# A hybrid HGRN2 and stick-breaking block: FFN and embedding stores issued on ScalarE's DMA queue

## The chip, the cores and the metric

The kernel runs on one core of a Trainium2 chip. The core has TensorE (PE in the profile, with PEld for its weight loads), VectorE (DVE), ScalarE (ACT), GpSimd (POOL) and SyncE (SP), and 16 DMA engines that serve all of its queues. The metric is the device time of one execution in microseconds; the time before is the median of three runs.

## The reference

One layer of a decoder trunk on 2048 tokens of width 1024. What is computed, cut to its core:

```python
u = rmsnorm(h, attn_pre_norm)
hq, hf, hi, hg, sq, sk, sv = split(u @ w_in)
o_hg = rmsnorm(hgrn2_mix(hq, hf, hi, lb), hg_out_norm) * silu(hg)    # 4 heads, recurrent
o_sb = rmsnorm(stick_breaking_mix(sq, sk, sv), sb_out_norm)          # 8 heads, causal
h = h + rmsnorm(concat([o_hg, o_sb]) @ w_out, attn_post_norm)
u = rmsnorm(h, ffn_pre_norm)
gate, up = split(u @ w_gate_up)                                      # 1024 -> 2 x 2816
y = (silu(gate) * up) @ w_down                                       # 2816 -> 1024
h = h + rmsnorm(y, ffn_post_norm)
h = h + (p @ ple_proj) * sigmoid(h @ ple_gate)                       # p: 2048 x 256
```

All of it is in float32. The change touches what comes behind the attention heads: part of the residual before the feed-forward network (FFN), the FFN, and the gated per-layer embedding.

## The kernel before

**Stages.** The first 1500 us hold the input projection, the two kinds of heads and most of the output projection. Behind them a `Drive` runs six lists of steps in order: `gate_up(0)`, `down(0)`, `gate_up(1)`, `down(1)`, `ple(0)`, `ple(1)`. The number is a pair of token groups (1024 tokens, in two groups of 512). Each step has a `prepare` (loads and splits of weights) and a `run` (matmuls); `Drive` prepares three to five steps ahead. Side work hangs on the steps as hooks: `post_late` (residual of the last group, L717), `turner` (transposes of normalised rows, L752), `down_combos` and `ple_combos` (combinations of weight blocks, L834), `make_pt` (transposes of `p`, L775), `post_y` and `turn_y` (residual of the FFN and its transposes, L1079 and L1089).

**Arithmetic.** A float32 matrix product is done with three matmuls of rounded operands: `pair_of` has ScalarE round a tile (`wh` or `uh`, L811), and VectorE or GpSimd takes the remainder (`wl` or `ul`, L812); `mm3` issues the three matmuls (L223 to L225). Each large product goes block by block with the seven products of a Strassen-like scheme, in the order 1, 2, 6, 3, 7, 5, 4 (`CHAIN`); `chain` adds them up from PSUM. The blocks' sums and differences go through the helpers `sub` and `add`, so they appear as L816 and L819.

**What passes through DRAM.** `gate_up` works in 11 column blocks for each pair; at the end of each block it forms the seven operands of the hidden layer that `down` needs and stores them in `hid_s` (five at L1016, two at L1021). `down_combos` and `ple_combos` store the combinations of `w_down` and `ple_gate`. `post_y` stores the residual stream in `h2_s`, `turn_y` its transposes in `h2t_s`, and `ple` the result.

**Queues and order.** Every DMA, load or store, is issued by SyncE in one order. Weights and reloaded tiles come through `load` (L796) into 12 slots `wr`; a load waits until its slot is free, which is when the last operation on the tile before is done, mostly the subtraction of L812. TensorE's order is that of the program. The order of the other engines, and each DMA's completion semaphore out of eight, is set by the framework's scheduler as it builds the program. A DMA waits for what it reads or overwrites, and for the landing of the DMA that used its semaphore before.

**PSUM.** TensorE's transposes in `turner`, `make_pt` and in `turn_y` for one group of each pair share one bank, `hg`. ScalarE takes their result out (L751 for `turner`, L1088 for `turn_y`), and the next transposes wait for that.

Of the kernel before, what the change touches and what calls it, by code (L numbers as in the profile page):

```python
# [15 lines left out]
P = 128  # L16
# [72 lines left out]
def hybrid_block(  # L89
# [6 lines left out]
    nc = tc.nc  # L96
    ctx.enter_context(tc.manual_schedule(engines={mybir.EngineType.PE}))
    x, p, out = x[0], p[0, 0], out[0]
# [16 lines left out]
    h_s = scratch("h_s", (GT, D))  # L115
    h2_s = scratch("h2_s", (GT, D))
# [3 lines left out]
    pt_s = scratch("pt_s", (PLE // P, P, GT))  # L120
# [8 lines left out]
    def ctile(name, shape, dt=F32, pool=const):  # L129
# [9 lines left out]
        out=maskneg, in_=maskneg, compare_op=ALU.is_gt, fill=-1e30, base=0,  # L139
# [566 lines left out]
    def post_late(g):  # L706

        for t in range(TT):
            rows = slice(t * P, (t + 1) * P)
            ss = const.tile([P, 2], F32, tag="ss", name="ss", bufs=8)  # L710
            for j in range(2):
                cs = slice(j * GT, (j + 1) * GT)
                m, h = load(h2_s[g][rows, cs]), load(x[g * GT + t * P:g * GT + (t + 1) * P, cs])
                gb = load(attn_post_norm[0:1][:, cs].to_broadcast((P, GT)))
                nc.vector.scalar_tensor_tensor(m, m, rows_m[t], gb, op0=ALU.mult, op1=ALU.mult)
                nc.gpsimd.tensor_tensor(h, h, m, op=ALU.add)
                nc.sync.dma_start(h_s[g][rows, cs], h)  # L717
                nc.scalar.activation(junk, h, AF.Square, accum_out=ss[:, j:j + 1])
                if j == 1:
                    row_rstd(None, rows_h[t], ss)  # L720
                yield

    def turn(src, dst, gain, tag, new_in, new_out, scales=None):

        def get(q):
            ts = []
            for i in range(2):
                r = new_in().rearrange("p (t d) -> p t d", t=2)
                rows = src[2 * i * P:2 * (i + 1) * P, q * 256:(q + 1) * 256]
                nc.sync.dma_start(r, rows.rearrange("(t p) d -> p t d", p=P))  # L730
                for n in range(2):
                    if scales:
                        nc.scalar.activation(r[:, n, :], r[:, n, :], AF.Copy, scale=scales[2 * i + n])
                    ts.append(r[:, n, :])
            return ts

        nxt = get(0)
        yield
        for q in range(4):
            ts = nxt  # L740
            nxt = get(q + 1) if q < 3 else None
            for c in range(2):
                b = bank(tag)
                for t in range(TT):
                    nc.tensor.transpose(b[:, t * P:(t + 1) * P], ts[t][:, c * P:(c + 1) * P], ident)
                e = new_out()
                k = 2 * q + c
                if gain is None:
                    nc.scalar.copy(e, b)
                else:  # L750
                    nc.scalar.activation(e, b, AF.Copy, scale=gain[:, k:k + 1])  # L751
                nc.sync.dma_start(dst[k], e)  # L752
                yield

    def make_pt():
        def get(n):
            raw = load(p[2 * n * P:2 * (n + 1) * P, :].rearrange("(t p) d -> p t d", p=P),
                       lambda r: r.rearrange("p (t d) -> p t d", t=2))
            return raw.rearrange("p (t d) -> p t d", t=2)

        nxt = get(0)
        yield
        for n in range(NG * TT // 2):
            raw = nxt
            nxt = get(n + 1) if n + 1 < NG * TT // 2 else None
            b = bank("hg")
            for t in range(2):
                for c in range(PLE // P):
                    nc.tensor.transpose(
                        b[:, (c * 2 + t) * P:(c * 2 + t + 1) * P], raw[:, t, c * P:(c + 1) * P], ident)  # L770
            e = acc("pt")
            nc.scalar.copy(e, b)
            g, i = divmod(n, TT // 2)
            for c in range(PLE // P):
                nc.sync.dma_start(pt_s[g][c][:, 2 * i * P:2 * (i + 1) * P], e[:, c * 2 * P:(c + 1) * 2 * P])  # L775
            yield


# [51 lines left out]
    def combos(blk, dst, e):  # L830
        t = [load(blk(i, j)) for i, j in ((0, 0), (0, 1), (1, 0), (1, 1))]
        b_combos(*t, e)
        for i, r in zip((1, 3, 4, 2), t):
            nc.sync.dma_start(dst[i - 1], r)  # L834

    wd_s = [dram.tile([4, P, GT], F32, tag=f"wd_s{k}", name=f"wd_s{k}") for k in range(DFF // 256)]
    wp_s = [dram.tile([4, P, GT], F32, tag=f"wp_s{k}", name=f"wp_s{k}") for k in range(ND // 2)]
# [115 lines left out]
    def gate_up(grp, tt):  # L953
        def block(fb):
            s = {}
            cs = [{}, {}]

            def wload(i, j):
                out = []
                for n in range(2):  # L960
                    r = slice((4 * j + 2 * n) * P, (4 * j + 2 * n + 2) * P)
                    c0 = i * DFF + fb * 256
                    out.append(load(w_gate_up[r, c0:c0 + 256].rearrange("(k p) n -> p k n", p=P),
                                    lambda r: r.rearrange("p (k n) -> p k n", k=2)))
                return out

            def prepare(prod):
                if prod == 1:
                    w = wload(0, 0)
                elif prod == 2:  # L970
                    w = wload(0, 1)
                elif prod == 6:
                    w, a21, a22 = wload(0, 0), wload(1, 0), wload(1, 1)
                    s["s1"] = [xt("s1") for _ in range(2)]
                    s["s3"] = [xt("s3") for _ in range(2)]
                    for n in range(2):
                        add(V, s["s1"][n], a21[n], a22[n])
                        sub(V, s["s3"][n], w[n], a21[n])
                        sub(V, w[n], s["s1"][n], w[n])
                    s["s2"] = w  # L980
                elif prod == 3:
                    w = wload(0, 1)
                    for n in range(2):
                        sub(V, w[n], w[n], s["s2"][n])
                elif prod == 7:
                    w = s["s3"]
                elif prod == 5:
                    w = s["s1"]
                else:
                    w = wload(1, 1)  # L990
                s[prod] = [pair_of(t, "w", prod, V if n or prod in (6, 3) else G) for n, t in enumerate(w)]

            def gated(j):
                for q in range(2):
                    sg = acc("sg")
                    nc.scalar.activation(sg, cs[q][1, j], AF.Sigmoid)
                    nc.vector.tensor_tensor(sg, cs[q][1, j], sg, op=ALU.mult)
                    nc.vector.tensor_tensor(cs[q][2, j], cs[q][2, j], sg, op=ALU.mult)

            def run(prod):  # L1000
                for q in range(2):
                    b = mm_bank()
                    for k in range(ND // 2):
                        o = (k % 2) * 256 + q * P
                        mm3(b, [t[:, o:o + P] for t in s[prod][k // 2]], tt[prod, k], k == 0, k == ND // 2 - 1)
                    chain(prod, cs[q], b, new_gu)
                if prod == 5:
                    gated(2)
                if prod == 4:
                    gated(1)  # L1010
                    h11, h12, h21, h22 = cs[0][2, 1], cs[1][2, 1], cs[0][2, 2], cs[1][2, 2]
                    s1, s3 = acc("hs"), acc("hs")
                    add(V, s1, h21, h22)
                    sub(V, s3, h11, h21)
                    for i, t in ((1, h11), (2, h12), (4, h22), (5, s1), (7, s3)):
                        nc.sync.dma_start(hid_s[grp][fb, i - 1], t)  # L1016
                    s2, s4 = acc("hs"), acc("hs")
                    sub(V, s2, s1, h11)
                    sub(V, s4, h12, s2)
                    for i, t in ((6, s2), (3, s4)):  # L1020
                        nc.sync.dma_start(hid_s[grp][fb, i - 1], t)  # L1021

            return {prod: (lambda p=prod: prepare(p), lambda p=prod: run(p)) for prod in CHAIN}

# [45 lines left out]
    def post_y(g, i):  # L1070
        halves = ready[g][i]
        r = row_rstd(halves)
        for j, t in enumerate(halves):
# [2 lines left out]
            nc.vector.scalar_tensor_tensor(t, t, r, gy, op0=ALU.mult, op1=ALU.mult)  # L1076
            hr = load(h_s[g][i * P:(i + 1) * P, cs])
            add(G, t, t, hr)
            nc.sync.dma_start(h2_s[g][i * P:(i + 1) * P, cs], t)  # L1079

    def turn_y(g, i, tag):

        for j, t in enumerate(ready[g][i]):
            b = bank(tag)
            for c in range(TT):
                nc.tensor.transpose(b[:, c * P:(c + 1) * P], t[:, c * P:(c + 1) * P], ident)
            e = acc("ht")
            nc.scalar.copy(e, b)  # L1088
            nc.sync.dma_start(  # L1089
                h2t_s[g][TT * j:TT * (j + 1), :, i * P:(i + 1) * P].rearrange("k p t -> p k t"),  # L1090
                e.rearrange("p (k t) -> p k t", k=TT))

# [1 line left out]
    def ple(grp, ss):  # L1094
# [29 lines left out]
        def run_p(half, i):  # L1124
            for j in range(2):
# [7 lines left out]
                hr = load(h2_s[g0 + half][i * P:(i + 1) * P, c])  # L1133
                add(G, y, y, hr)
                r0 = (g0 + half) * GT + i * P
                nc.sync.dma_start(out[r0:r0 + P, c], y)

        def none():
            pass
# [154 lines left out]
        return slot("wr", 0, "wr")  # L1294

    def turner(src, dst, gain, scales=None):
        return turn(src, dst, gain, "hg", wr, acc, scales)

    for k in range(ND // 2):
        at(0, k, lambda k=k: t_second(0, tt0, k))  # L1300
# [48 lines left out]
```

## Time and profile before

| what | value |
|---|---|
| median of three runs | 3060.1 us (3058.16 to 3062.44) |
| the profiled execution's own time | 3057.24 us |
| its span | 3055.5 us |
| granted TensorE clock | 0.99 |
| DMA, mean over the span | 197 GB/s |
| chain that ended last | PE 41%, DMA 6%, DVE 5%, POOL 3%, issue 3%, ACT 1% |

The page is read from the busy shares of the engines to the stretches of time in which they stand idle. `L834 <- DVE wr L816: 34.9, 28, 3.9` in a list of waits means: ahead of line 834 the engine named first was idle for 34.9 us in all, 28 times, 3.9 us at the longest, and what ended it was VectorE's operation of line 816 on tile `wr`. In a timeline a row gives start, duration, engine, line, operation, output and inputs, and in brackets the idle time before it with its releaser. In a table by windows, the busy time of PE, PEld, DVE, ACT and POOL is followed by the granted clock (1.00 is full speed), the busy share of the 16 DMA engines and what they moved. The costliest groups of the page, to show the form (busy time, mean ns of one, idle time before and its main releaser):

```profile
L811 ACT CAST wh<-wr 128x512 fp32r<-128x512 f32 x600 | 352.8, 618 | 473.4 <-PE mm L224 192.5
L812 POOL TENSOR_TENSOR wl<-wr,wh 128x512 fp32r<-128x512 f32 x256 | 370.6, 1453 | 460.8 <-ACT wh L811 427.1
L223 PE MATMUL mm<-uh,wh 128*128 128x512 f32 x1168 | 482.4, 413 | 1.9 <-DVE eb L336 1.6
```

### The profile page before, as it was taken

The numbers are of one execution on the slowest core, as the hardware profiler recorded it, in microseconds if no ns is written. First come the engines' busy times: TensorE is split into PE (matmuls) and PEld (weight loads), VectorE is DVE, ScalarE is ACT, GpSimd is POOL, SyncE is SP. The second block draws the span as 40 slices with busy tenths as digits, with TensorE's granted clock in tenths as the row PEclk, the third lists the DMA queues.
The fourth block names the chain that finished last, engine by engine and source line by source line (L and its number), as shares of the span: only waits on it lengthen the run. The fifth ranks groups of instructions, "written<-read, shape, count | busy, mean of one in ns | idle before, by whom it ended". The sixth has DMA issues, their size and how long they took to land.

```text
span 3055.5 us, 52953 instructions
## 1 busy us (share of the span) xinstructions
PE 2920.4 (96%) x18280; PEld 2425.4 (79%) x18280; DVE 2065.6 (68%) x2917; ACT 1583.7 (52%) x3188; POOL 1463.9 (48%) x1490
## 2 busy tenths in 40 slices
PE   8999999999999998888998999999999999999989
PEld 6888787878787787778886878888788888878767
DVE  3556666677677776745787787655877776656674
ACT  5666656666666666757633233455433333545442
POOL 3344455545556665857522223455732221456564
PEclk9999999999999999999999999999999999999999
DMA  7765565455445444447867767667955555677974
GB/s 216 219 213 164 160 183 164 145 158 164 142 139 155 143 136 135 158 154 253 302 213 236 263 211 248 215 196 220 340 188 169 173 172 175 209 217 244 309 248 138
DMA packets 469420, 602.28 MB, mean 197 GB/s; under 512 B 43168, under 2 KB 277664, under 8 KB 469152
## 3 DMA queue, kind: packets, MB, share of 16 engines
q1 hardware_dynamic: 469152, 598.91, 61.9%
q8 instruction: 144, 2.36, 0.3%
q14 instruction: 124, 1.02, 0.1%
HBM read 439.89 MB, written 158.86 MB: 196 GB/s over the span
## 4 chain that ended last, share of the span: by engine, by line
PE 41%; DMA 6%; DVE 5%; POOL 3%; issue 3%; ACT 1%; SPq 0%; POOLq 0%; ACTq 0%; DVEq 0%
PE mm L223 6%; PE mm L224 6%; PE mm L225 6%; PE z L225 4%; PE z L223 4%; PE z L224 4%; PE tr L223 2%; PE tr L224 2%; PE tr L225 2%; PE av L225 2%; PE av L224 2%; PE av L223 2%; DMA wr<-in_w_gate_up_dram 1%; DVE wr L816 1%; DMA wr<-in_ffn_post_norm_dram 1%
## 5 line engine op out<-in xcount | busy, mean ns | idle before, releaser
L811 ACT CAST wh<-wr 128x512 fp32r<-128x512 f32 x600 | 352.8, 618 | 473.4 <-PE mm L224 192.5
L812 POOL TENSOR_TENSOR wl<-wr,wh 128x512 fp32r<-128x512 f32 x256 | 370.6, 1453 | 460.8 <-ACT wh L811 427.1
L435 POOL TENSOR_TENSOR a<-be,ring 128x512 f32<-128x512 f32 (+2 forms) x320 | 318.4, 995 | 431.0 <-DVE ring L431 410.5
L223 PE MATMUL mm<-uh,wh 128*128 128x512 f32 x1168 | 482.4, 413 | 1.9 <-DVE eb L336 1.6
L225 PE MATMUL mm<-uh,wl 128*128 128x512 f32 x1168 | 458.9, 393 | 0.0
L224 PE MATMUL mm<-ul,wh 128*128 128x512 f32 x1168 | 457.1, 391 | 0.0
L812 DVE TENSOR_TENSOR wl<-wr,wh 128x512 fp32r<-128x512 f32 x344 | 299.2, 877 | 181.8 <-ACT wh L811 166.1
L431 DVE TENSOR_TENSOR_SCAN ring<-z,ring,be 128x512 f32<-128x512 f32 x192 | 245.6, 1279 | 114.6 <-ACT z L417 111.6
L223 PE MATMUL mm<-wh,uh 128*128 128x256 f32 (+1 forms) x992 | 308.6, 311 | 1.0 <-DVE vv L350 1.0
L224 PE MATMUL mm<-wl,uh 128*128 128x256 f32 (+1 forms) x992 | 293.7, 296 | 6.7 <-POOL wl L812 6.7
L225 PE MATMUL mm<-wh,ul 128*128 128x256 f32 (+1 forms) x992 | 293.6, 296 | 0.0
L225 PEld LDWEIGHTS mm<-uh,wl 128*128 128x128 f32 x1168 | 219.4, 188 | 50.6
L223 PEld LDWEIGHTS mm<-uh,wh 128*128 128x128 f32 x1168 | 220.5, 189 | 43.7 <-DVE eb L336 2.1
L448 DVE TENSOR_TENSOR al<-tr,ah 128x512 fp32r<-128x512 f32 (+1 forms) x320 | 192.1, 600 | 91.4 <-ACT ah L446 90.8
L224 PEld LDWEIGHTS mm<-ul,wh 128*128 128x128 f32 x1168 | 220.8, 189 | 39.4
L209 ACT CAST wh<-wr 128x512 fp32r<-128x512 f32 x288 | 178.2, 619 | 133.9 <-PE mm L224 80.2
L210 POOL TENSOR_TENSOR wl<-wr,wh 128x512 fp32r<-128x512 f32 x144 | 188.9, 1311 | 100.2 <-ACT wh L209 97.0
L812 POOL TENSOR_TENSOR wl<-s,wh 128x512 fp32r<-128x512 f32 x44 | 97.0, 2211 | 270.8 <-ACT wh L811 242.0
L446 ACT CAST ah<-tr 128x512 fp32r<-128x512 f32 (+1 forms) x320 | 167.6, 524 | 110.6 <-PE tr L443 107.9
L416 ACT ACTIVATE be<-z 128x512 f32<-128x512 f32 (+2 forms) x320 | 171.0, 535 | 90.4 <-PE z L410 40.6
L224 PEld LDWEIGHTS mm<-wl,uh 128*128 128x128 f32 x992 | 191.9, 193 | 12.2 <-POOL wl L812 7.1
L223 PEld LDWEIGHTS mm<-wh,uh 128*128 128x128 f32 x992 | 191.5, 193 | 9.1 <-issue 1.2
(305 smaller groups left out, 7270.0 us busy)
## 6 DMA issues: line engine op xcount, KB each, us to landing
wr<-in_w_gate_up_dram SPq DMA_DIRECT2D x308, 256.0 KB, 3.7
wr<-in_w_in_dram SPq DMA_DIRECT2D x224, 256.0 KB, 3.1
wr<-hid_s SPq DMA_DIRECT2D x154, 256.0 KB, 2.9
wr<-in_w_down_dram SPq DMA_DIRECT2D x110, 256.0 KB, 3.4
hid_s<-hs SPq DMA_DIRECT2D x88, 256.0 KB, 3.5
wr<-wd_s SPq DMA_DIRECT2D x88, 256.0 KB, 3.1
kt<-k_s SPq DMA_DIRECT2D x80, 256.0 KB, 3.0
vt<-v_s SPq DMA_DIRECT2D x80, 256.0 KB, 3.2
```

What stands on the lines that cost most here:

```text
L209: nc.scalar.copy(hi, src)
L210: (lo_engine or nc.gpsimd).tensor_tensor(lo, src, hi.bitcast(F32), op=ALU.subtract)
L223: nc.tensor.matmul(o, l[0], r[0], start=start, stop=False)
L224: nc.tensor.matmul(o, l[0], r[1], start=False, stop=False)
L225: nc.tensor.matmul(o, l[1], r[0], start=False, stop=stop)
L416: nc.scalar.activation(be[:, :n], z[:, :n], AF.Sigmoid, scale=0.125)
L431: nc.vector.tensor_tensor_scan(r[:, o:o + n][:, ::-1], z[:, :n][:, ::-1], be[:, :n][:, ::-1], init, op0=ALU.mult, op1=ALU.bypass)
L435: nc.gpsimd.tensor_tensor(a[:, :n], be[:, :n], r[:, o + 1:o + n + 1], op=ALU.mult)
L446: nc.scalar.copy(hi[:, lo_c:], tr[:, lo_c:])
L448: nc.vector.tensor_tensor(lo[:, lo_c:], tr[:, lo_c:], hi[:, lo_c:].bitcast(F32), op=ALU.subtract)
L811: nc.scalar.copy(hi, src)
L812: lo_engine.tensor_tensor(lo, src, hi.bitcast(F32), op=ALU.subtract)
```

## The change

Ten edits replace SyncE as the issuer of stores by ScalarE. `turn` gets a parameter for it, which `turner` sets; the calls of `turn` in the output projection keep SyncE.

```diff
@@ post_late @@
-                nc.sync.dma_start(h_s[g][rows, cs], h)
+                nc.scalar.dma_start(h_s[g][rows, cs], h)
@@ turn @@
-    def turn(src, dst, gain, tag, new_in, new_out, scales=None):
+    def turn(src, dst, gain, tag, new_in, new_out, scales=None, store=nc.sync):
...
-                nc.sync.dma_start(dst[k], e)
+                store.dma_start(dst[k], e)
@@ make_pt @@
-                nc.sync.dma_start(pt_s[g][c][:, 2 * i * P:2 * (i + 1) * P], e[:, c * 2 * P:(c + 1) * 2 * P])
+                nc.scalar.dma_start(pt_s[g][c][:, 2 * i * P:2 * (i + 1) * P], e[:, c * 2 * P:(c + 1) * 2 * P])
@@ combos @@
-            nc.sync.dma_start(dst[i - 1], r)
+            nc.scalar.dma_start(dst[i - 1], r)
@@ gate_up, run @@
                     for i, t in ((1, h11), (2, h12), (4, h22), (5, s1), (7, s3)):
-                        nc.sync.dma_start(hid_s[grp][fb, i - 1], t)
+                        nc.scalar.dma_start(hid_s[grp][fb, i - 1], t)
...
                     for i, t in ((6, s2), (3, s4)):
-                        nc.sync.dma_start(hid_s[grp][fb, i - 1], t)
+                        nc.scalar.dma_start(hid_s[grp][fb, i - 1], t)
@@ post_y @@
-            nc.sync.dma_start(h2_s[g][i * P:(i + 1) * P, cs], t)
+            nc.scalar.dma_start(h2_s[g][i * P:(i + 1) * P, cs], t)
@@ turn_y @@
-            nc.sync.dma_start(
+            nc.scalar.dma_start(
@@ ple, run_p @@
-                nc.sync.dma_start(out[r0:r0 + P, c], y)
+                nc.scalar.dma_start(out[r0:r0 + P, c], y)
@@ turner @@
-        return turn(src, dst, gain, "hg", wr, acc, scales)
+        return turn(src, dst, gain, "hg", wr, acc, scales, nc.scalar)
```

SyncE issues 2442 DMAs before and 2092 now; 350 go to ScalarE. TensorE's order is the same. Three places of ScalarE's order follow, as pieces of the difference (+ is new; the numbers in names tell tiles apart).

First, ScalarE in `gate_up(0)`, near 1670 us of the profile, where a block of the hidden layer ends; `hs` are its sums, `acc` a transposed tile of `turner`, `s1` and `s3` sums of weights:

```order
 L811 CAST wh_21422<-s3_21300 128x512
+L1016 DMA hid_s0_111<-cu_20987 128x512
 L926 COPY cu_21416<-z_21403 128x512
+L1016 DMA hid_s0_111<-cu_21002 128x512
+L834 DMA wd_s3_239<-wr_21520 128x512
+L1016 DMA hid_s0_111<-hs_21351 128x512
+L1016 DMA hid_s0_111<-hs_21352 128x512
+L834 DMA wd_s3_239<-wr_21518 128x512
 L811 CAST wh_21478<-s1_21297 128x512
+L1021 DMA hid_s0_111<-hs_21360 128x512
 L751 ACTIVATE acc_21371<-hg_21366,g_ffn_172 128x512
```

Five stores of the hidden layer and two of `wd_s` now stand between the cast `wh_21422` and the eviction of the bank `hg` at L751.

Second, ScalarE at the end of `down(0)`, near 2185 us; `c22` and `cu` are the residual tiles that GpSimd's addition completes, `ht` their transposes:

```order
 L811 CAST wh_26371<-s1_26195 128x512
+L1079 DMA h2_s1_92<-cu_24282 128x512
 L811 CAST wh_26375<-s1_26196 128x512
+L1079 DMA h2_s1_92<-c22_25775 128x512
+L1079 DMA h2_s1_92<-cu_24287 128x512
+L1079 DMA h2_s1_92<-c22_25781 128x512
 L1088 COPY ht_26434<-hg_26429 128x512
+L1079 DMA h2_s1_92<-cu_24292 128x512
+L1089 DMA h2t_s1_104<-ht_26434 128x4x128
 L1088 COPY ht_26442<-hg_26437 128x512
```

Four stores of residual tiles, of later rows than those being transposed, now come ahead of the first eviction `ht_26434`.

Third, ScalarE at the end of `down(1)`, near 2843 us, with the same names for the other pair; the activation of L1130 is a sigmoid of `ple`:

```order
 L926 COPY cu_32529<-mm_32516 128x512
+L1079 DMA h2_s3_94<-cu_30490 128x512
 L926 COPY cu_32590<-av_32577 128x512
+L1079 DMA h2_s3_94<-c22_31984 128x512
+L1079 DMA h2_s3_94<-cu_30495 128x512
 L1088 COPY ht_32634<-hg_32629 128x512
 L1130 ACTIVATE c11_32627<-c11_32627 128x512
 L811 CAST wh_32555<-wr_32553 128x512
```

Here three stores come ahead of the first eviction `ht_32634`.

## The prediction

> **What bounds the kernel now.** I read the page's first part, then the windows by stage, then the waits of SyncE's queue and of TensorE, then the timeline where TensorE stands still.
>
> ```profile
> span 3055.5 us, 52953 instructions
> PE 2920.4 (96%) x18280; PEld 2425.4 (79%) x18280; DVE 2065.6 (68%) x2917; ACT 1583.7 (52%) x3188; POOL 1463.9 (48%) x1490
> ```
>
> TensorE is busy for 96% of the span. The first store that changes queue is issued at about 1540 us, so what counts is the time behind 1497 us.
>
> ```profile
> 1497.00:1800.00 303.00, 282.08 (x1208) 227.91 (x1207) 251.78 (x356) 95.97 (x179) 84.10 (x65) 0.96 0.71 229
> 1800.00:2212.00 412.00, 408.13 (x1810) 331.93 (x1809) 285.09 (x385) 190.29 (x352) 201.90 (x142) 1.00 0.74 240
> 2212.00:2620.00 408.00, 408.00 (x1788) 333.17 (x1787) 306.18 (x456) 132.16 (x223) 105.75 (x63) 1.00 0.55 179
> 2620.00:2870.00 250.00, 243.89 (x1077) 196.56 (x1077) 146.92 (x171) 130.46 (x246) 148.41 (x120) 1.00 0.77 247
> 2870.00:3056.00 186.00, 171.39 (x722) 136.85 (x720) 116.00 (x148) 63.19 (x112) 100.36 (x71) 0.97 0.61 204
> ```
>
> The columns are window, length, busy time of PE, PEld, DVE, ACT and POOL, granted clock, DMA share, GB/s. TensorE's idle time here is 20.9 + 3.9 + 0 + 6.1 + 14.6 = 45.5 us. The clock costs 303×0.04 + 186×0.03 = 17.7 us more (an estimate). So at most some 63 us can be won; nothing of the kind limits what can be lost. ScalarE is busy for 612 of these 1559 us.
>
> Does SyncE's order of stores hold its loads back? Its waits, from 1497 us on (total, times, longest):
>
> ```profile
> SPq L796 <- DVE wl L812: 305.0, 249, 6.8
> SPq L796 <- POOL wl L812: 245.3, 159, 10.2
> SPq L834 <- DVE wr L816: 34.9, 28, 3.9
> SPq L1016 <- DVE c L998: 17.1, 17, 3.1
> SPq L1021 <- DVE hs L816: 15.9, 19, 2.5
> ```
>
> Loads (L796) wait 550 us for a free `wr` slot, which the subtraction at L812 gives back. The largest rows of stores sum to 68 us; a load behind such a store would often have met a slot wait next. So the queue is mostly held by slots, not by stores.
>
> **The change, part by part.** 350 stores leave SyncE for ScalarE: 60 of L834, 154 of the hidden products (110 L1016, 44 L1021), 32 each of L1079, L1089 and L1136, 16 each of L752 and L775, 8 of L717. Each carries its wait with it. On SyncE a store that waits for VectorE or GpSimd holds only loads; on ScalarE, which takes its instructions in order, it holds the casts (L811) and the evictions of PSUM behind it. In the built program each DMA also waits for the landing of the previous one on its completion semaphore, and eight of these serve both queues.
>
> *Issuing itself.*
>
> ```profile
> 1682.51 0.43 SPq L1021 DMA_DIRECT2D hid_s<-hs  x1
> 2188.20 0.38 SPq L1079 DMA_DIRECT2D h_s<-c  x1
> 1776.84 2.85 SPq L834 DMA_DIRECT2D wd_s<-wr  x3
> ```
>
> One costs SyncE 0.38 to 0.95 us; ScalarE's price is not in this trace. I take 0.4, so 350 × 0.4 = 140 us beside ScalarE's 947 idle us: nothing by itself. At 0.95 it would be 330 us, still inside, but each burst of four then holds an eviction by 2 us more; that end goes into the upper bounds below.
>
> *Casts held in gate_up.* In the blocks the order puts stores that wait for VectorE ahead of casts. The worst one:
>
> ```profile
> 1762.98 0.62 ACT L811 CAST wh<-wr 128x512 fp32r<-128x512 f32 x1
> 1779.86 0.68 DVE L816 TENSOR_TENSOR wr<-wr 128x512 f32<-128x512 f32 x1
> 1786.78 0.39 PE L223 MATMUL mm<-uh,wh 128*128 128x512 f32 x1
> ```
>
> This cast comes behind three stores of L834, which need the combinations that end near 1779.3, and so falls some 16.7 us later; GpSimd's L812 then ends near 1782. Matched in program order, the first matmul that uses it starts at 1786.78. Covered, with about 4 us left. Other casts slip by 5 us or so against leads of 13 to 20. I charge +2 for the stretch (0 to +8).
>
> *Place A, the one long gap.* L1016 and L1021 stand ahead of the L751 eviction.
>
> ```profile
> 1677.43 0.69 ACT L751 ACTIVATE acc<-hg,g_ffn 128x512 f32<-128x512 f32 x1 [5.68 <-DVE cu L998]
> 1678.17 1.11 PE L745 MATMUL hg<-ident,wr 128*128 128x128 f32 x4 [10.31 <-ACT acc L751]
> 1680.93 0.68 DVE L816 TENSOR_TENSOR hs<-hs,cu 128x512 f32<-128x512 f32 x1
> 1650.00:1700.00 50.00, 39.69 (x173) 32.22 (x172) 34.73 (x51) 14.83 (x28) 10.78 (x10) 0.90 0.72 236
> ```
>
> TensorE waits 10.31 us for the single `hg` bank. The store ahead of that eviction needs the `hs` that ends at 1681.61, so the eviction starts at about 1681.95 in place of 1677.43: +4.5. Earlier loads take back up to 2.8. I take **+3** (0 to +5).
>
> *Place B, the transition from down(0) to gate_up(1).* Ahead of `ht_26434` now stand L1079 stores, which need GpSimd's adds.
>
> ```profile
> 2186.64 0.59 ACT L1088 COPY ht<-hg 128x512 f32<-128x512 f32 x1 [4.29 <-PE hg L1086]
> 2187.37 0.63 PE L1086 MATMUL hg<-ident,c 128*128 128x128 f32 x4 [0.77 <-ACT ht L1088]
> 2187.82 1.30 POOL L819 TENSOR_TENSOR cu<-cu,wr 128x512 f32<-128x512 f32 x1 [0.63 <-DVE cu L1076]
> 2190.41 1.29 POOL L819 TENSOR_TENSOR c<-c,wr 128x512 f32<-128x512 f32 x1 [1.29 <-DVE c L1076]
> 2180.00:2190.00 10.00, 9.23 (x45) 7.48 (x44) 10.00 (x10) 3.52 (x7) 7.86 (x6) 1.00 1.02 335
> ```
>
> The second of these adds ends at 2191.70, its store is issued by 2192.05, and the eviction follows: 5.4 us behind 2186.64. TensorE's next step is four transposes into the bank that it frees, so the 5.4 show in full. The later pairs share this lag rather than add to it. But VectorE is busy for all of the 10 us, and what slips on ScalarE (casts, whose results VectorE and GpSimd take) can slip a second time: 10.8. I take **+9** (+3 to +11), nearer to the upper end because no engine here has slack to catch up with.
>
> *Place C, down(1) to ple(0)*, is built in the same way, with less before it.
>
> ```profile
> 2843.72 0.59 ACT L1088 COPY ht<-hg 128x512 f32<-128x512 f32 x1 [2.64 <-PE hg L1086]
> 2843.48 1.72 POOL L819 TENSOR_TENSOR cu<-cu,wr 128x512 f32<-128x512 f32 x1
> 2840.00:2850.00 10.00, 8.29 (x44) 6.57 (x44) 6.20 (x8) 5.59 (x11) 9.38 (x7) 1.00 1.05 383
> hid_s<-hs SPq DMA_DIRECT2D x88, 256.0 KB, 3.5
> h2t_s<-ht SPq DMA_DIRECT2D x32, 256.0 KB, 5.5
> ```
>
> The add ends at 2845.20, so the first eviction moves by at least 1.8 us. If its store must also await a landing of its semaphore's previous DMA, issued near 2844 and 3.5 to 5.5 us under way, by about 4 or more. GpSimd is at 94%, so a second slip is likely here too: **+6** (+2 to +12).
>
> *The clock.* Place A's gap goes with a granted clock of 0.90 over 50 us, so 5 us lost. New gaps of about half that length at B and C may drop it once, or in several places: **+5** (0 to +15). The Trainium skill, "TensorE: Matmul & The Clock Gate", "Part 1: The HAM clock gate", says that an idle window of about 3.4 us halves the clock. By that rule the gaps of 5.4 us at B and some 4 us at C would each do so, this term would be nearer to +10 and the sum +28 (an estimate from that page); no gap of that length at B or C stands in this trace to show it, only the one of 10.31 us.
>
> *What is won.* SyncE's loads no longer stand behind stores. Laid on the times of before, they move by some tenths of a us on average and by 3 to 5 at single places, because the slot wait comes next. What hides the gain is that wait; if it were gone, the 63 us above would be the limit. I take **−2** (0 to −15).
>
> **Sum.** 2 + 3 + 9 + 6 + 5 − 2 = +23 us. The profiled execution took 3057.24 us (span 3055.5), 2.9 below the median of the runs, 3060.1. So 3080 there, and **3083 us** on the median.
>
> **The rivals.**
>
> *No change: 3060 us.* The lags fall into slack: only 612 of 1559 us of ScalarE are used, and wh's lead is long. It is also what comes out if the stores merely change queue and the shared semaphores keep the order as it was. For it: TensorE idles for 0 us in 2212:2620. Against: the `ht` evictions, which have a single bank and no lead. By the Trainium skill, "DMA: Bandwidth & Descriptors", "Issuing engines are not separate DMA queues", another engine's queue uses the same 16 DMA engines and saves only issue time; by that rule alone the time would stay. The trace agrees on the engines' being full (share 1.02 at place B), but shows a wait that the rule doesn't speak of.
>
> *Faster: 3040 us.* The mechanism is SyncE's head of line at place A.
>
> ```profile
> 1646.45 10.66 SPq L796 DMA_DIRECT2D wr<-in_w_gate_up_dram  x7
> 1654.82 0.69 DVE L819 TENSOR_TENSOR s<-wr 128x512 f32<-128x512 f32 x1 [6.78 <-DMA wr<-in_w_gate_up_dram]
> ```
>
> VectorE waited 6.78 us there for a load, and its late products led to the 10.31 us gap. If the loads came over 5 us earlier, the gap and its clock (10.3 + 5.0) would go, and a few us in like places: −20. It decides if stores rather than slots hold the queue; the 550 us of slot waits speak against it, and ScalarE's new waits at the same gap.
>
> *Much slower: 3170 us.* ScalarE is held in each of the 22 gate_up blocks beyond the leads; with 5 us a block, +110. For it: the cover of 4 us at 1786.78. Against: the other leads of 13 us and more.
>
> **How the numbers follow.** My forecast (slower, 3066 to 3112) has 0.62, much slower 0.08, no change 0.16, faster 0.14. Faster or slower means by over 0.2%, 6 us, about what a measurement of this kernel can tell from no change: 0.14 / 0.16 / 0.70. The terms' low ends sum to 0+0+3+2+0−15 = −10 and their high ends to 8+5+11+12+15 = +51, so 3050 to 3111. I take **3050 to 3112**: it leaves out much slower and the deep half of faster, about 0.17.
>
> **What would show it.** Right: at L1088 and L751 ScalarE's idle time is ended by L1079's and L1016's waits; TensorE's waits rise from
>
> ```profile
> PE hg L745 <- ACT acc L751: 13.1, 2, 10.3
> PE hg L1086 <- ACT ht L1088: 6.3, 7, 1.5
> ```
>
> to 16 and to 15 or more; TensorE loses busy share in 2180 to 2212 and 2840 to 2870; SyncE's waits for `wl` stay near 550 us. Wrong: those two waits stay as they are and the gap of 10.31 us shrinks (faster); or TensorE waits for `wl` in many blocks between 1800 and 2600 (much slower); or GpSimd's and VectorE's adds move earlier, so that the stores on ScalarE find them done (no change).

## The result and the profile after

The changed kernel took 3080.22 us (median of four runs, 3076.69 to 3084.55) against 3061.27 us before (four runs): 1.0057 times as long, 95% interval 1.0041 to 1.0073. The profiled execution took 3076.69 us, 19.5 us more than that of before. The forecast was 3083.

The page of the changed kernel: the span, the busy times, the two queues, and the issues of one of the moved stores.

```profile
span 3074.9 us, 52909 instructions
PE 2926.8 (95%) x18280; PEld 2429.1 (79%) x18280; DVE 2058.5 (67%) x2917; ACT 1584.4 (52%) x3188; POOL 1467.8 (48%) x1490
q1 hardware_dynamic: 406464, 509.23, 54.0%
q10 hardware_dynamic: 62688, 89.68, 8.1%
hid_s<-hs ACTq DMA_DIRECT2D x88, 256.0 KB, 4.0
```

No engine got noticeably more work. A second queue, ScalarE's (q10), now carries 89.68 MB. The time must be in waits. Here is the changed kernel by windows, with the columns as before:

```profile
1497.00:1800.00 303.00, 287.87 (x1242) 233.03 (x1241) 248.82 (x366) 101.85 (x189) 102.45 (x70) 0.98 0.73 237
2620.00:2870.00 250.00, 241.29 (x1052) 194.83 (x1052) 143.22 (x171) 126.98 (x241) 145.23 (x119) 0.99 0.77 248
2870.00:3076.00 206.00, 184.57 (x777) 147.07 (x775) 121.85 (x155) 68.76 (x122) 103.52 (x74) 0.95 0.59 192
2190.00:2200.00 10.00, 7.02 (x23) 5.80 (x24) 5.94 (x8) 2.31 (x4) 7.20 (x5) 0.66 0.94 319
2830.00:2840.00 10.00, 6.33 (x27) 4.84 (x26) 6.31 (x8) 4.39 (x9) 6.64 (x5) 0.81 1.03 345
2840.00:2850.00 10.00, 10.00 (x39) 7.98 (x38) 5.02 (x7) 8.50 (x23) 7.98 (x13) 0.84 1.07 372
```

Two opposite things stand here: in gate_up(0) TensorE is busier than before (287.87 against 282.08 us of the same 303), and at the two transitions and in the last window it is not, with the clock down to 0.66, 0.81 and 0.84 over ten microseconds each.

The sharpest view is a comparison of the two traces. Both hold the same 18,280 matmuls in the same order, so the start of each, after minus before, is a curve; its steps say where time went. This table was worked out in that way, for the changed kernel:

| stretch of before, us | place | lag gained, us |
|---|---|---|
| 0 to 1540 | nothing changed here | +3.0 |
| 1540 to 1800 | gate_up(0), with place A | −6.2 |
| 1800 to 2160 | down(0) | −0.3 |
| 2160 to 2300 | place B | +10.7 |
| 2300 to 2780 | gate_up(1), down(1) | −0.7 |
| 2780 to 2880 | place C | +7.0 |
| 2880 to 3000 | ple(0) to ple(1), call it place D | +6.1 |
| whole | | +19.6 |

A stretch in which a run moves nothing still comes out up to some 3 us off (only_hid below, +2.8 at C), so smaller differences of one stretch are not read.

Place B, from the timeline of the changed kernel:

```profile
2190.59 1.26 POOL L819 TENSOR_TENSOR c<-c,wr 128x512 f32<-128x512 f32 x1 [1.29 <-DVE c L1076]
...
2191.88 0.33 ACTq L1079 DMA_DIRECT2D h_s<-c  x1
2192.25 0.59 ACT L1088 COPY ht<-hg 128x512 f32<-128x512 f32 x1 [7.13 <-POOL c L819]
...
2192.98 1.09 PE L1086 MATMUL hg<-ident,c 128*128 128x128 f32 x4 [6.84 <-ACT ht L1088]
```

GpSimd's addition ends at 2191.85, the store of its result is issued at 2191.88, and only then ScalarE takes the bank out. TensorE waits 6.84 us for it. (The trace leaves digits out of names: h_s at L1079 is h2_s.)

Place D, which the prediction charged with nothing:

```profile
2937.84 6.72 ACTq L1136 DMA_DIRECT2D out_dram<-c  x4
...
2946.44 1.14 ACT L811 CAST uh<-wr 128x512 fp32r<-128x512 f32 x2 [10.47 <-DMA out_dram<-c]
...
2959.37 1.14 ACT L811 CAST uh<-wr 128x512 fp32r<-128x512 f32 x2 [9.70 <-POOL c L819]
...
2961.60 0.80 PE L223 MATMUL mm<-wh,uh 128*128 128x512 f32 x1 [4.49 <-ACT wh L811]
```

ScalarE stands for 10.47 and 9.70 us behind stores of the result, with casts for ple(1) queued behind them, and TensorE waits 4.49 us for such a cast.

Two things end ScalarE's new idle time: GpSimd's results, and landings of DMAs. From its list of waits behind 1475 us, three of the latter kind:

```profile
ACT wh L811 <- DMA wd_s<-wr: 15.7, 3, 7.2
ACT wh L811 <- DMA hid_s<-hs: 13.6, 4, 4.5
ACT uh L811 <- DMA out_dram<-c: 10.5, 1, 10.5
```

Those casts read none of these. Added up over all rows of the kind behind 1540 us, landings of stores ended 17.1 us of ScalarE's idle time before (7 times) and 112.2 us after (30 times). This is idle time of ScalarE and not loss of TensorE: back_y below has 60.5 us of it and is no slower than before.

### The profile page after: what moved, and what is told of

It is laid out like the page before. It is cut to its first block, busy times and chain, and to the rows that moved or that the text cites. A ratio compares the mean times of both kernels' runs of the same rounds, so it can differ in the third digit from the quotient of the medians.

```text
span 3074.9 us, 52909 instructions
## 1 busy us (share of the span) xinstructions
PE 2926.8 (95%) x18280; PEld 2429.1 (79%) x18280; DVE 2058.5 (67%) x2917; ACT 1584.4 (52%) x3188; POOL 1467.8 (48%) x1490
## 3 DMA queue, kind: packets, MB, share of 16 engines
q10 hardware_dynamic: 62688, 89.68, 8.1%
## 4 chain that ended last, share of the span: by engine, by line
PE 41%; DMA 7%; POOL 4%; DVE 3%; issue 3%; ACT 2%; SPq 0%; ACTq 0%; POOLq 0%; DVEq 0%
PE mm L223 6%; PE mm L224 5%; PE mm L225 5%; PE z L225 4%; PE z L223 4%; PE z L224 4%; PE tr L223 2%; PE tr L225 2%; PE tr L224 2%; PE av L223 2%; PE av L225 2%; PE av L224 2%; DMA wr<-h_s 1%; POOL c L819 1%; POOL wl L812 1%
## 5 line engine op out<-in xcount | busy, mean ns | idle before, releaser
L812 POOL TENSOR_TENSOR wl<-wr,wh 128x512 fp32r<-128x512 f32 x256 | 365.2, 1431 | 482.7 <-ACT wh L811 416.7
L223 PE MATMUL mm<-uh,wh 128*128 128x512 f32 x1168 | 484.5, 415 | 4.0 <-DVE eb L336 1.8
L812 DVE TENSOR_TENSOR wl<-wr,wh 128x512 fp32r<-128x512 f32 x344 | 295.2, 865 | 200.7 <-ACT wh L811 183.6
L223 PE MATMUL mm<-wh,uh 128*128 128x256 f32 (+1 forms) x992 | 309.4, 312 | 4.5 <-ACT wh L811 4.5
L223 PEld LDWEIGHTS mm<-uh,wh 128*128 128x128 f32 x1168 | 221.6, 190 | 46.6 <-DVE eb L336 2.2
L812 POOL TENSOR_TENSOR wl<-s,wh 128x512 fp32r<-128x512 f32 x44 | 102.4, 2332 | 300.6 <-ACT wh L811 276.7
L223 PEld LDWEIGHTS mm<-wh,uh 128*128 128x128 f32 x992 | 191.6, 193 | 12.9 <-ACT wh L811 4.9
```

Of the source, the lines that this page charges most:

```text
L223: nc.tensor.matmul(o, l[0], r[0], start=start, stop=False)
L812: lo_engine.tensor_tensor(lo, src, hi.bitcast(F32), op=ALU.subtract)
```

## The experiments

Two theories stood at the outset: a store that waits for its producer holds ScalarE (the prediction's), or each moved store costs the same for its issue and its place on the shared semaphores. Each run was compared with the kernel before on the same chip, in five rounds. The stretches below are those of the table above, each from one profiled execution; the last column holds for medians.

| run | 1540 to 1800 | B | C | D | ratio to before (95%) |
|---|---|---|---|---|---|
| the change | −6.2 | +10.7 | +7.0 | +6.1 | 1.0057 (1.0041 to 1.0073) |
| back_h2 | −10.4 | +7.1 | +9.3 | +3.7 | 1.0049 (1.0036 to 1.0061) |
| back_out | −7.2 | +10.8 | +7.0 | −1.2 | 1.0031 (1.0019 to 1.0042) |
| back_both | −6.8 | +10.3 | +10.1 | −0.2 | 1.0041 (1.0027 to 1.0055) |
| h2_late | −5.8 | +9.3 | +8.9 | +4.5 | 1.0049 (1.0036 to 1.0062) |
| only_own | −1.3 | +7.8 | +9.1 | −1.5 | 1.0051 (1.0036 to 1.0065) |
| only_h2 | +2.6 | +10.8 | +8.3 | −0.4 | 1.0062 (1.0048 to 1.0075) |
| only_gu | −8.0 | −0.7 | −0.3 | +0.3 | 0.9969 (0.9957 to 0.9981) |
| back_y | −5.6 | +0.7 | −0.3 | −0.5 | 0.9984 (0.9974 to 0.9994) |
| only_hid | −7.7 | −0.2 | +2.8 | −1.4 | 0.9983 (0.9970 to 0.9996) |
| only_comb | −6.8 | +0.2 | −0.8 | −1.4 | 0.9980 (0.9968 to 0.9992) |
| only_h2t | +1.4 | +8.6 | +9.7 | +0.2 | 1.0057 (1.0043 to 1.0072) |
| h2t_later | +2.2 | +4.1 | +7.9 | −2.2 | 1.0020 (1.0010 to 1.0029) |

**First group: take stores back from the changed kernel.**

back_h2:

```diff
-            nc.scalar.dma_start(h2_s[g][i * P:(i + 1) * P, cs], t)
+            nc.sync.dma_start(h2_s[g][i * P:(i + 1) * P, cs], t)
```

> The changed kernel with the 32 stores of L1079 (the residual after the FFN) issued on SyncE again; the other 318 stay on ScalarE. Theory (a store that waits on ScalarE for GpSimd's addition holds the evictions and casts behind it): the loss at the end of down(0) (10.6 us between the two profiles) goes, and most of that at the end of down(1) (6.8), so 14 to 17 us less than the changed kernel, about 1.0005 of before (1.000 to 1.002). Rival (each moved store costs its issue and its place on the shared completion semaphores, 19.6 us over 350 stores, 0.056 us each): 1.8 us less, about 1.005 of before.

Measured 3074.52 us, 1.0049: the theory falls in its simple form. Place B still costs 7.1 us and C 9.3, though no store waits for GpSimd there any more. The rival's figure, 1.005, fits this run.

back_out:

```diff
-                nc.scalar.dma_start(out[r0:r0 + P, c], y)
+                nc.sync.dma_start(out[r0:r0 + P, c], y)
```

> The changed kernel with the 32 stores of the result (L1136) issued on SyncE again. Theory: the ScalarE idle stretches of 10.47 and 9.70 us behind L1136's stores near 2946 and 2959 us go, and with them the 4.5 us wait of TensorE for a cast; 5 to 6 us less than the changed kernel, about 1.004 of before. Rival (equal price for each store): 1.8 us less, about 1.005. The two lie close: the profile decides, by whether TensorE's wait at L223 for ScalarE's cast near 2961 us is gone.

Measured 3071.73 us, 1.0031, below the figure of either theory, the first one's being still inside the interval. The wait at L223 for ScalarE's cast is gone from TensorE's list, and D's +6.1 is −1.2. The five other runs with L1136 on SyncE and L1079 or L1089 on ScalarE (back_both, only_own, only_h2, only_h2t, h2t_later) have no loss at D either. Place D is due to L1136.

back_both carries both edits.

> The changed kernel with both L1079 and L1136 issued on SyncE again, 286 stores on ScalarE. Theory: 19 to 23 us less than the changed kernel, and the 5.7 us that gate_up(0) gained stay: 0.998 to 1.000 of before. Rival (equal price): 3.6 us less, about 1.0045.

Measured 3073.29 us, 1.0041. D is clean, B and C are as bad as ever (+10.3, +10.1). It has fewer stores on ScalarE than back_out and is no faster, which speaks against an equal price for each store. The figure of that theory, 1.0045, lies inside the interval, though; what rules it out comes below, a gain with 214 stores (only_gu) and the whole loss with 32 (only_h2t).

h2_late keeps all 350 stores on ScalarE, but puts those of L1079 behind the evictions of their own rows:

```diff
@@ post_y @@
-            nc.scalar.dma_start(h2_s[g][i * P:(i + 1) * P, cs], t)
@@ turn_y @@
-            nc.scalar.copy(e, b)
+            last = nc.scalar.copy(e, b)
...
+        with tc.issue_after(last.ins):
+            [nc.scalar.dma_start(h2_s[g][i * P:(i + 1) * P, j * GT:(j + 1) * GT], t) for j, t in enumerate(ready[g][i])]
```

> All 350 stores on ScalarE's queue, but the 32 of L1079 are issued by turn_y behind the evictions of the transposes of the same rows, so that GpSimd's addition is done when ScalarE comes to them. Number of stores, queue and bytes are those of the changed kernel; only the wait for GpSimd is gone. Theory (the wait is what costs): as with the stores back on SyncE, 13 to 17 us less than the changed kernel, 1.000 to 1.002 of before. Rival (issue, queue or shared semaphores cost): no change, 1.0057.

Measured 3074.97 us, 1.0049: again no better than back_h2. With GpSimd's results no longer awaited, something else holds ScalarE at B and C. The trace of back_h2 and ScalarE's landings above pointed at L1089, whose stores still were on ScalarE in all four runs.

**Second group: put single stores on ScalarE in the kernel before.** The theories now: only producers cost, or landings cost too. Each run takes over only the lines of the change that are named.

only_own: L752, L775 and L1089.

> The kernel before with only those stores on ScalarE whose tile ScalarE itself has just written: L752, L775, L1089, 64 in all. No such store waits for another engine's result; what it can wait for is the landing of the DMA that used its completion semaphore before, which is one of SyncE's in most cases. Producers' theory (only the wait for GpSimd's or VectorE's result costs): 1.000 of before. Landings' theory (ScalarE is held until DMAs of SyncE's queue have landed): slower, 1.002 to 1.004, with TensorE's gaps at the end of down(0) and down(1) as in the run with L1079 back on SyncE, and over 30 us of ScalarE's idle time ended by landings of stores or loads that its next operation doesn't read.

Measured 3078.65 us, 1.0051, a little beyond the range for landings: stores that wait for no other engine's result lose nearly all that the change loses.

only_h2: L1079.

> The kernel before with only the 32 stores of L1079 on ScalarE. Producers' theory: the whole loss of the two transitions, 14 to 17 us, 1.0045 to 1.0055. Landings' theory: the stores wait for landings as well, but L1089's no longer hold ScalarE; about half, 1.002 to 1.004. The eviction ht near 2186 us should come behind GpSimd's addition in both, 5 to 6 us later than before.

Measured 3080.00 us, 1.0062. In this profile ScalarE's evictions at L1088 wait 9.4 us for GpSimd's additions. TensorE's longest wait at B ends with such an eviction:

```profile
2208.53 0.40 ACTq L1079 DMA_DIRECT2D h_s<-c  x1
2208.97 0.59 ACT L1088 COPY ht<-hg 128x512 f32<-128x512 f32 x1 [6.82 <-POOL c L819]
...
2209.70 1.09 PE L1086 MATMUL hg<-ident,c 128*128 128x128 f32 x4 [7.54 <-ACT ht L1088]
```

So a producer's wait is enough for most of B's loss without L1089. The run doesn't take landings out: the stores of L1079 await them too (landings of stores end 28.4 us of ScalarE's idle time here, 17.1 before). The two causes don't add: B costs 10.7 us with both lines on ScalarE, 10.8 with L1079 alone, 7.1 with L1079 taken back. Why they don't is not shown.

only_gu: L834, L1016 and L1021.

> The kernel before with only the 214 stores inside gate_up on ScalarE (L834, L1016, L1021). Both theories: the 6 us that every changed profile so far gained near 1765 us (a gap of 2.9 us and the half clock behind it are gone) are kept and nothing is lost later: 0.998 of before (0.9975 to 0.9995). If a price for each store (0.056 us) held: 1.004.

Measured 3052.93 us, 0.9969: faster than both kernels, 27 us below the changed one. TensorE's list of waits behind 1540 us, for this run:

```profile
PE hg L745 <- ACT acc L751: 10.8, 1, 10.8
PE mm L224 <- POOL wl L812: 7.0, 1, 7.0
PE hg L1086 <- ACT ht L1088: 5.5, 7, 0.8
```

The evictions of L1088 are awaited for 0.8 us at most, as before.

back_y: the changed kernel with L1079, L1089 and L1136 on SyncE.

> The changed kernel with L1079, L1089 and L1136 on SyncE again: no store of post_y, turn_y and the result is on ScalarE, 254 others are. Both theories: nothing holds ScalarE at the transitions, so the losses there (10.7 and 7 us, and 4 to 6 near 2940) go: 0.998 to 1.000 of before. If SyncE's queue, relieved of the earlier stores, is itself what shifts the transitions, they stay and it is 1.003 or more.

Measured 3056.09 us, 0.9984. With both kinds of store gone from ScalarE at the transitions, B is at +0.7 and C at −0.3. SyncE's relief doesn't shift the transitions by itself. From back_both this run differs in L1089 alone, and is at 0.9984 where that was at 1.0041.

**Third group: which store, and why.**

only_h2t: L1089 alone.

> The kernel before with only the 32 stores of L1089 on ScalarE, each behind the eviction that writes its tile. Landings' theory: 15 to 18 us lost at the two transitions, as in the run with L752 and L775 too, 1.004 to 1.006. If L752 and L775 were what cost there: under 1.002.

Measured 3080.51 us, 1.0057: 32 stores, each of a tile that ScalarE itself has just written, cost as much as the whole change. The timeline of this run ahead of place B shows how:

```profile
2174.90 1.07 ACT L1088 COPY ht<-mm 128x512 f32<-128x512 f32 x2
2175.45 0.43 SPq L1079 DMA_DIRECT2D h_s<-c  x1
...
2179.48 1.83 ACTq L1089 DMA_DIRECT2D h2t_s<-ht  x2
2181.35 1.14 ACT L811 CAST wh<-wr 128x512 fp32r<-128x512 f32 x2 [5.38 <-DMA h_s<-c]
...
2182.52 1.36 DVE L812 TENSOR_TENSOR wl<-wr,wh 128x512 fp32r<-128x512 f32 x1 [6.09 <-ACT wh L811]
...
2185.90 0.57 ACT L1088 COPY ht<-mm 128x512 f32<-128x512 f32 x1
...
2186.52 0.50 PE L223 MATMUL mm<-uh,wh 128*128 128x512 f32 x1 [3.06 <-ACT ht L1088]
```

ScalarE's evictions end at 2175.97, and their two stores could go at once. The first goes at 2179.48, the second at 2180.94. As built, a store of L1089 waits for ScalarE's copy (Activation) and for the last landing on its own completion semaphore, one of the eight (DMAHW) that both queues share. ScalarE's order at these rows:

```
L1088 COPY ht_26156<-mm_26151 128x512 [waits PE_49]
L1089 DMA h2t_s0_103<-ht_26148 128x4x128 [waits DMAHW2_49,Activation_49]
L1089 DMA h2t_s0_103<-ht_26156 128x4x128 [waits DMAHW4_49,Activation_49]
L811 CAST wh_26163<-wr_26159 128x512 [waits DVE_49]
```

By the semaphores in the trace, the first store awaited a load of `w_gate_up` into another tile, issued by SyncE at 2174.10 and landed at 2179.40; the second awaited the store of L1079 issued at 2175.45, which landed at 2180.86, 5.41 us later. That is a usual time for such a store, by the trace's answer on L1079:

```profile
DMA to landing us min/median/max: 2.4/5.0/6.0
```

It is not data: the stores read neither tile, and the cast's own tile, `wr_26159`, had landed at 2174.04. So the awaited DMA can be a load as well as a store; what counts is that it was issued late and shares the semaphore. In the profile of before, the same cast follows the evictions without a gap:

```profile
2167.15 1.20 ACT L811 CAST wh<-wr 128x512 fp32r<-128x512 f32 x2
```

This run is 8.4 us behind before at these rows, so 2167.15 would be 2175.5 here, and the cast starts 5.8 us late. VectorE's L812 waits for it; the eviction of 2185.90 is 4.6 us late by the same reckoning, and TensorE, which waits for that, 3.2 us.

h2t_later issues the same stores a row later:

```diff
-            nc.scalar.copy(e, b)
-            nc.sync.dma_start(
-                h2t_s[g][TT * j:TT * (j + 1), :, i * P:(i + 1) * P].rearrange("k p t -> p k t"),
-                e.rearrange("p (k t) -> p k t", k=TT))
+            last = nc.scalar.copy(e, b)
+            later.append((h2t_s[g][TT * j:TT * (j + 1), :, i * P:(i + 1) * P].rearrange("k p t -> p k t"),
+                          e.rearrange("p (k t) -> p k t", k=TT)))
+        with tc.issue_after(last.ins):
+            [nc.scalar.dma_start(*later.pop(0)) for _ in range(len(later) - (0 if i == TT - 1 else 2))]
+    later = []
```

> As the run with only L1089 on ScalarE, but each row's two stores are issued behind the evictions of the next row, so that more of SyncE's DMAs have landed when ScalarE comes to them. Number of stores and queue are the same. Landings' theory: ScalarE's idle time ended by landings at the transitions shrinks, and the time is 1.001 to 1.003 of before. If the issue itself or the queue cost: as with the stores in their old place, 1.004 to 1.006.

Measured 3069.14 us, 1.0020: some 11 us less than only_h2t with the same number of stores on the same queue. Issue time and the second queue are out as the main cause; what matters is what has landed when ScalarE comes to the store. Landings of stores end 23.3 us of ScalarE's idle time here against 36.4 in only_h2t, as that theory expected. Place B fell from 8.6 to 4.1, C only from 9.7 to 7.9; what keeps C up stays open.

only_hid: L1016 and L1021; only_comb: L834.

> The kernel before with only the 154 stores of the hidden layer on ScalarE (L1016, L1021). Theory of the gain near 1765 us: these stores hold ScalarE's casts of the tiles s, GpSimd's subtractions of them start later, and VectorE's step cu (L816), for which TensorE waited 2.9 us with the half clock behind it, runs at 0.7 us an operation in place of 1.75 and comes in time. Then the whole gain is here: 0.998 of before (0.997 to 0.999), VectorE's operations near 1760 us at 0.7 us, no gap of TensorE there. Rival (SyncE, relieved of stores, loads earlier): the gain is shared with the run of L834 by the number of stores, 0.9985 here.

> The kernel before with only the 60 stores of weight combinations on ScalarE (L834). Theory as above: TensorE's gap of 2.9 us near 1765 us stays; 1.000 of before (0.9990 to 1.0005). Rival (SyncE's relief): 0.999, with the gap smaller.

Measured 3056.63 us (0.9983) and 3054.24 us (0.9980). The theory of the gain falls: L834 alone should have brought nothing, and it lost TensorE's gap near 1765 us as well. In only_comb's timeline there (its first half ran 7 us later than that of before) VectorE still has operations of 1.78 us, and `cu` comes in time all the same:

```profile
1762.98 1.45 POOL L812 TENSOR_TENSOR wl<-s,wh 128x512 fp32r<-128x512 f32 x1 [3.22 <-ACT wh L811]
1763.20 1.78 DVE L998 TENSOR_TENSOR cu<-cu,sg 128x512 f32<-128x512 f32 x1
...
1766.61 0.67 DVE L816 TENSOR_TENSOR cu<-cu,z 128x512 f32<-128x512 f32 x1
1767.21 0.68 DVE L819 TENSOR_TENSOR hs<-c,c 128x512 f32<-128x512 f32 x1
```

Two things differ from before. VectorE waits less for loads: from 1545 to 1770 us its rows of waits for loads add up to 42.9 us before, 35.8 in only_comb, 31.1 in only_hid, 30.6 in only_gu, but 44.0 in only_h2t and 44.5 in only_h2, which left the stores of gate_up on SyncE. That is SyncE's relief, the rival. And the scheduler, which builds each kernel anew, put `cu` ahead of `hs` on VectorE in these runs. Before it was behind:

```profile
1764.76 1.75 DVE L819 TENSOR_TENSOR hs<-c,c 128x512 f32<-128x512 f32 x1
1766.42 0.67 DVE L816 TENSOR_TENSOR cu<-cu,z 128x512 f32<-128x512 f32 x1
...
1767.24 0.77 PE L223 MATMUL z<-uh,wh 128*128 128x512 f32 x1 [2.92 <-DVE cu L816]
```

In only_own the order is swapped while the loads are no earlier, and there the gap at this place shrank to 1.26 us. So the swap takes part at that place. How much of the gain in 1540 to 1800 is the swap's and how much the loads', stays open; no run had the swap alone with all stores on SyncE.

## Why the prediction held, point by point

**The total.** Forecast +23 us; measured 19 by the medians. From 1540 us on the curve rises by 16.6. Two steps missed and cancelled each other, which is luck: gate_up(0) was charged about +3 (2 + 3 − 2) and came out at −6.2, place D was charged nothing and cost 6.1.

**Place B, +9 and part of the clock:** right. The eviction was to follow at 2192.05, held by GpSimd's addition that ends at 2191.70; it came at 2192.25 behind one that ended at 2191.85. The lag rose by 10.7 us, of which some 2.5 is the clock (see below). So 8.2 stand against the +9. The Trainium skill, "TensorE: Matmul & The Clock Gate", "Part 1: The HAM clock gate", has the clock halved after an idle window of some 3.4 us; this trace agrees, with 0.66 over ten microseconds around the end of the gap of 6.84 us. A shorter gap can do it as well: in the trace of before half speed came with the gap of 2.92 us near 1765 (0.83 in two windows of ten microseconds). What the step did not see is that the wait for GpSimd is sufficient but not necessary: with it taken out, L1089's waits for landings hold casts and evictions there (+7.1 to +10.3).

**Place C, +6:** the size was about right (7.0, with some 2.8 us of it clock), the way only in part. The longest waits of TensorE there were for GpSimd's additions, not for the first eviction:

```profile
2829.74 2.18 ACT L811 CAST wh<-wr 128x512 fp32r<-128x512 f32 x4 [2.64 <-DMA h_s<-c]
...
2830.97 1.31 DVE L812 TENSOR_TENSOR wl<-wr,wh 128x512 fp32r<-128x512 f32 x1 [4.36 <-ACT wh L811]
...
2833.03 1.65 POOL L819 TENSOR_TENSOR c<-c,wr 128x512 f32<-128x512 f32 x1 [1.29 <-DVE c L1076]
...
2834.73 0.66 PE L1086 MATMUL mm<-ident,c 128*128 128x128 f32 x4 [1.42 <-POOL c L819]
...
2837.63 1.12 PE L1086 MATMUL mm<-ident,c 128*128 128x128 f32 x4 [2.24 <-POOL c L819]
```

A landing held a cast for 2.64 us; VectorE's L812 waited 4.36 us for that cast and then did the L1076 on which GpSimd's addition depends. So the second slip that the prediction named is there. Of the 7.0 us, 2.6 came with these two waits (before, one of 1.28 us stood there), and some 2.0 with the later evictions.

**Waits for landings** were the mis-sized term. The prediction gave them one sentence and a place in C's upper bound, "by about 4 or more". Landings of stores ended 112.2 us of ScalarE's idle time against 17.1, but much of that is harmless (60.5 us in back_y); where it falls is what counts. L1089 alone, which the prediction did not count as waiting for anything at B, makes the whole loss, with 36.4 us in only_h2t.

**Place A, +3:** wrong in sign. The gap before the transposes fell from 10.31 to 8.25 us. Why is not shown: in only_hid and only_gu, which move the same stores, it was 12.4 and 10.8 us, and in only_own, which leaves them on SyncE, 8.0.

**Casts in gate_up, +2, and SyncE's relief, −2:** the casts were covered, as said; TensorE's only wait for one is that of 4.49 us at D. The gain was larger: 1540 to 1800 fell by 6.2 us with place A in it. The slot waits stayed on top of SyncE's list and grew (384.4 and 277.4 us, in all 662 against 550), and still VectorE waited less for loads. The rival "faster" may have its mechanism right in part: the gain came mostly from the gap of 2.9 us near 1765 and the clock behind it, where the swap of `cu` and `hs` takes part, not from the gap of 10.31.

**The clock, +5:** about right. By the clock records behind 1540 us, TensorE worked at half speed for 15.2 us before and for 27.4 after, so it lost 7.6 and 13.7 us (an estimate, half of these times): +6.1. Of this 2.5 fall to B, 2.8 to C, 1.0 to D, 1.2 to place A and 1.7 to a place near 1625; the 3.1 near 1765 are gone.

**Place D, at nothing:** wrong. L1136 cost 6.1 us, by the mechanism of the prediction, in a place where it wasn't looked for.

**Issue time** was rightly set at nothing by itself: only_gu puts 214 stores on ScalarE and gains. The rival "no change" rested on what the Trainium skill, "DMA: Bandwidth & Descriptors", "Issuing engines are not separate DMA queues", states: another issuing engine saves issue time only. As to the load of the DMA engines this case agrees: the two queues took 54.0% and 8.1% of their time, the one queue 61.9% before. The time differs from it both ways (0.9969 and 1.0062), by waits of the issuing engine that the rule doesn't cover.

**The signs.** TensorE's waits for `ht` rose from 6.3 to 14.3 us, close to the 15 named. Those for `acc` at L745 were to rise from 13.1 to 16 and fell to 10.9. The waits of SyncE for `wl` were to stay near 550 us and came to 662. So the signs were right at the transitions and wrong in gate_up(0).

## What to carry to other kernels

A store moved to another engine's queue is not free because that engine is half idle: list what it waits for, the producer and the DMA that last used its completion semaphore, and what is queued behind it on the new engine; if the last of these is an eviction of a single bank, the wait shows in full (6.84 us of TensorE behind GpSimd's addition at B), and casts held by landings of 5 us cost TensorE 3.06 us at one place. Move stores where the new engine's work runs far ahead of its consumers (gate_up here, 0.9969), and leave them where it is just in time (the transitions, 1.006). Take a cause out singly and also put it in singly: back_h2 alone would have cleared L1079, only_h2 alone would have blamed it for everything, and both were needed to see two causes, each of them sufficient.

## What the runs showed beyond expectation

- The kernels are alike up to about 1540 us, and yet the profiles reach that point 1.6 to 9.4 us later than the profile of before did (13 profiles). Single profiles can't be compared by their ends below that; steps of the lag curve and medians can.
- VectorE's 128x512 operations of float32 take 0.68 us in one moment and 1.75 to 1.78 in the next, the slow ones here while GpSimd has a subtraction of its own under way (only_comb, L998 at 1763.20 against L998 at 1762.60). The Trainium skill, "SBUF — State Buffer", "Who interferes with whom", has a VectorE operation with two inputs in SBUF contend with a GpSimd one that reads SBUF; these rows agree.
- A store issued by ScalarE occupies its queue for 0.33 to 0.47 us in the rows of place B (1 to 2 us for two where a wait lies between), about what it took on SyncE.
